# Second passes of a head's two widest score products, each on one half of the array's rows and side by side

## The chip, the core and the metric

The kernel runs on one core of one Trainium2 chip. What is measured is the device time of one execution in microseconds (us). TensorE (PE) multiplies matrices, VectorE (DVE), ScalarE (ACT) and GpSimd (POOL) do the rest, and SyncE (SP) issues every DMA of this kernel from one queue, in the order in which they stand there. A change of over 0.2% either way is about the least that a measurement of this kernel can tell from none.

## What is computed

A decoder trunk of two layers over 512 tokens of width 1024, with 16 heads of 64 dimensions. Layer 0 mixes by stick-breaking attention, layer 1 by dilated softmax attention; each is followed by a SwiGLU feed-forward stage. What matters here are the scores, of which both layers have the same kind:

```
z = jnp.einsum('bhqd,bhkd->bhqk', qb, kh).astype(jnp.float32) * scale   # layer 0, queries in blocks of 128
z = jnp.einsum('brhnqd,brhnkd->brhnqk', qb, k_band).astype(jnp.float32) * scale   # layer 1
```

Both are causal: of the four blocks of 128 queries, block i needs the scores of the first 128 (i + 1) keys alone.

## The kernel before, in words

All operands are float32 numbers kept as two float32r parts, a high and a low one. A product of two such numbers is three products of parts (high by high, high by low, low by high), added up in one PSUM bank; the weights of the model are split in this way on ACT and DVE while they stream in (`raw` tiles, split into `whi` and `wlo`).

For the scores the two parts of a head's 64 dimensions are laid on top of each other. `to_stationary` builds a tile `sta` (`STA[h]`) by DMA, with the high part of the queries in rows 0 to 63 and the low part in rows 64 to 127. `to_moving` builds a tile `mov` (`MOV[h]`) with the keys, high part and low part beside each other, the same in both halves of the rows. So one product on all 128 rows gives the queries' high and low part times one part of the keys at once, and two passes (keys high, keys low) give all four products, low by low among them. Both tiles are made for a pair of heads at a time, by 4 DMAs of `sta` and 4 of `mov`; they come from `hl`, the split query or key projection of the pair. In layer 1 the projection is first rotated (`rope`), which for all pairs but the first takes 4 more DMAs (`rp`) and a product on POOL.

The function `scores(h, u, beside)` issues the score products of one of three units of a head: unit 0 is query block 3 with 512 columns, unit 1 is block 2 with 384, unit 2 is blocks 1 and 0 together. Each unit takes one of three PSUM banks `z`, in turn. `stick_breaking` and `softmax` call it as the first thing of the step W0, W1 or W2 and then turn the scores into weights on ACT and DVE. The order of the steps of a head is written out in `PLAN`: for layer 0 it is T0 W0 F T1 F W1 A0 T2 F A1 W2 F A2, for layer 1 W0 T0 T1 W1 F W2 F A0 T2 F F A1 A2. T are transposes of the weights of the head before (`t<-cst,w` in layer 0, `t<-cst,z` in layer 1), A its products with the values (`av`), and F is filler: pieces of the projections of later heads (`pj`). That order sets priorities; a scheduler then settles the order on each engine by what it expects to be ready, so that a few instructions stand elsewhere than they were written.

Of the kernel before, what the change touches and what calls it, by code (L numbers as in the profile page):

```python
# [7 lines left out]
F = mybir.dt.float32  # L8
# [320 lines left out]
def trunk(ctx, tc, xg, wflat, cst_d, cs_d, outT):  # L329
    nc = tc.nc  # L330
    pe, act, dve, pool, sp = nc.tensor, nc.scalar, nc.vector, nc.gpsimd, nc.sync
# [26 lines left out]
    def T(name, dt=F, k=1):  # L358
        shape = [128, 512] if k == 1 else [128, k, 512]
        return rings["pool"].tile(shape, dt, name=name, bufs=rings["n"][name])  # L360
# [9 lines left out]
    def zb():  # L370
        return ps.tile([128, 512], F, name="z", bufs=3)
# [14 lines left out]
    def mm(out, a, b, start, stop):  # L386
        pe.matmul(out, a, b, start=start, stop=stop, skip_group_check=True)  # L387
# [141 lines left out]
    def to_stationary(p, hl):  # L529
        for i in range(2):  # L530
            t = T("sta", FR)
            for j in range(2):
                sp.dma_start(t[64 * j:64 * j + 64, :].bitcast(F), hl[64 * i:64 * i + 64, j, :].bitcast(F))
            STA[2 * p + i] = t

    def scaled(p):
# [26 lines left out]
    def sta_pieces(layer, p):  # L563

        return proj_pieces(lambda b: to_stationary(p, split_base(position(layer, b, p), 0.125)))
# [60 lines left out]

    UNITS = [[(3, 0, 512)], [(2, 0, 384)], [(1, 0, 256), (0, 256, 256)]]

    def scores(h, u, beside):
        k, q = MOV[h], STA[h]  # L630
        b = zb()
        for j, (i, o, n) in enumerate(UNITS[u]):
            lhs = q[:, 128 * i:128 * i + 128]
            if i == 0 and beside:

                mm(b[:, o:o + 256].rearrange("p (e n) -> p e n", e=2), lhs, k[:, :, :128], False, True)
                continue
            mm(b[:, o:o + n], lhs, k[:, 0, :n], j == 0, False)
            mm(b[:, o:o + n], lhs, k[:, 1, :n], False, True)
        return b  # L640

    def stick_breaking(h, u):

        b = scores(h, u, True)
        n = sum(128 * (i + 1) for i, _, _ in UNITS[u])
        stay, w = T("z"), T("w")
        if u == 2:
            act.activation(stay[:, 384:512], b[:, 384:512], AF.Copy)
            dve.tensor_add(b[:, 256:384], b[:, 256:384], stay[:, 384:512])
        act.activation(stay[:, :n], b[:, :n], AF.Sigmoid, scale=-1.0)  # L650
        act.activation(w[:, :n], b[:, :n], AF.Sigmoid)

        pool.memset(w[:, 128 * (UNITS[u][0][0] + 1) - 1:n:128], 0.0)
        res = {}
        for i, o, _ in UNITS[u]:
            e = o + 128 * (i + 1)
            back = stay[:, o:e][:, ::-1]

            dve.tensor_tensor_scan(back, back, diag[:, 512 - (e - o):][:, ::-1], 0.0, OP.mult, OP.add)
            dve.tensor_mul(w[:, o:e - 1], stay[:, o + 1:e], w[:, o:e - 1])  # L660
            res[i] = w[:, o:e]
        return res

    def softmax(h, u):

        b = scores(h, u, True)
        t = T("z")
        st = sb.tile([128, 4, 2], F, name="st", bufs=6)
        m = len(UNITS[u])
        res = {}  # L670
        for j, (i, o, _) in enumerate(UNITS[u]):
            n = 128 * (i + 1)
            res[i] = t[:, o:o + n]
            m_i = maskB[:, 512 - n:512]
            if i == 0:
                m_i = t[:, o + n:o + 2 * n]
                dve.tensor_add(m_i, b[:, o + n:o + 2 * n], maskB[:, 384:512])
            dve.tensor_tensor_reduce(res[i], b[:, o:o + n], m_i, scale=1.0,
                                     scalar=-3.0e38, op0=OP.add, op1=OP.max, accum_out=st[:, 0, j:j + 1])
        dve.tensor_scalar(st[:, 1, :m], st[:, 0, :m], -1.0, None, op0=OP.mult)  # L680
        for j, (i, _, _) in enumerate(UNITS[u]):
            act.activation(res[i], res[i], AF.Exp, bias=st[:, 1, j:j + 1], accum_out=st[:, 2, j:j + 1])
        dve.reciprocal(st[:, 3, :m], st[:, 2, :m])
        for j, (i, _, _) in enumerate(UNITS[u]):
            if u in DVE_UNITS:
                dve.tensor_scalar(res[i], res[i], st[:, 3, j:j + 1], None, op0=OP.mult)
            else:
                act.activation(res[i], res[i], AF.Copy, scale=st[:, 3, j:j + 1])
        return res
# [60 lines left out]
    def mixer(layer, slot0, gain_next):  # L750
        vslot = lambda p: (slot0 + p) % 9
        oslot = lambda p: (slot0 + 8 + p) % 9
        with phase(f"at{layer}", B_RINGS if layer else A_RINGS):
            def whole(fs_done):
                for f in fs_done[0]:
# [3 lines left out]
            pair = [pjbank(), pjbank()]  # L759
            both("qk", pair)  # L760
            ends = [lambda: to_stationary(0, split_base(position(layer, pair[0], 0), 0.125)),
                    lambda: to_moving(0, split_base(position(layer, pair[1], 0), 1.0))]
            v_first, v_last = v_pieces(0, vslot, zbank)
# [394 lines left out]
```

## Time and profile before

| | |
|---|---|
| median of 3 runs | 1211.41 us (1210.93 to 1211.87) |
| profiled execution | 1214.94 us |
| its span, first to last instruction | 1213.0 us |
| PE busy | 1188.7 us, 98% of the span |
| attention of layer 0 / layer 1, from its first score product on | 37.7 to 228 us / 630 to 826 us |
| score products (`z<-mov,sta`) | 7 a head, 224 in all |

PE's matmuls are pipelined: the recorded durations of neighbours overlap, and the time that one takes of a busy PE is read from its start to the start of the next. In the timeline neighbours of one kind are merged into a row ("x2"), whose first number is the start of the first, and whose second goes to the end of the last. Ends of matmuls are modelled by the profiler.

### The profile page before, as it was taken

The numbers are of one execution on the slowest core, as the hardware profiler recorded it, in microseconds if no ns is written. First come the engines' busy times: TensorE is split into PE (matmuls) and PEld (weight loads), VectorE is DVE, ScalarE is ACT, GpSimd is POOL, SyncE is SP. The second block draws the span as 40 slices with busy tenths as digits, with TensorE's granted clock in tenths as the row PEclk, the third lists the DMA queues.
The fourth block names the chain that finished last, engine by engine and source line by source line (L and its number), as shares of the span: only waits on it lengthen the run. The fifth ranks groups of instructions, "written<-read, shape, count | busy, mean of one in ns | idle before, by whom it ended". The sixth has DMA issues, their size and how long they took to land.

```text
span 1213.0 us, 21104 instructions
## 1 busy us (share of the span) xinstructions
PE 1188.7 (98%) x7501; PEld 1062.5 (88%) x7501; DVE 1013.3 (84%) x1831; ACT 697.2 (57%) x1331; POOL 169.9 (14%) x237
## 2 busy tenths in 40 slices
PE   9999999999999999999999999999999999999997
PEld 7989988888999999998788888888889999999996
DVE  6799899899987878786768899788899878787865
ACT  6667676675544444454466677767755444444443
POOL 0000000001100000014134343110111000000111
PEclk9999999999999999999999999999999999999998
DMA  7654644234242333332154546551343333332122
GB/s 263 179 144 117 154 118 118 62 104 139 89 139 85 109 94 114 90 111 79 35 140 131 155 130 172 144 148 53 96 140 113 114 102 108 91 119 88 44 62 70
DMA packets 74360, 138.30 MB, mean 114 GB/s; under 512 B 9616, under 2 KB 13712, under 8 KB 74256
## 3 DMA queue, kind: packets, MB, share of 16 engines
q1 hardware_dynamic: 74256, 136.97, 39.4%
q8 instruction: 59, 0.97, 0.3%
q14 instruction: 45, 0.37, 0.1%
HBM read 106.00 MB, written 2.10 MB: 89 GB/s over the span
## 4 chain that ended last, share of the span: by engine, by line
PE 86%; DVE 6%; DMA 2%; ACT 2%; issue 2%; POOL 1%; SPq 0%; POOLq 0%; DVEq 0%
PE pj L387 40%; PE z L387 29%; PE t L387 11%; PE av L387 3%; PE t L700 3%; DMA mov<-hl 1%; DMA raw<-wflat 1%; DVE w2lo L307 1%; DVE wlo L307 1%; DVE H L748 1%; ACT whi L306 0%; DVE ACC L441 0%; POOL up L963 0%; DMA H<-xg 0%; POOL H L1071 0%
## 5 line engine op out<-in xcount | busy, mean ns | idle before, releaser
L306 ACT ACTIVATE whi<-raw 128x512 fp32r<-128x512 f32 (+1 forms) x290 | 178.2, 620 | 135.6 <-PE pj L387 53.7
L307 DVE TENSOR_TENSOR wlo<-raw,whi 128x512 fp32r<-128x512 f32 (+1 forms) x290 | 203.6, 710 | 26.7 <-ACT whi L306 24.5
L387 PE MATMUL pj<-VO,whi 128*128 128x512 f32 x568 | 180.7, 398 | 2.0 <-DVE H L748 2.0
L387 PE MATMUL pj<-X,whi 128*128 128x512 f32 x512 | 165.0, 402 | 1.7 <-DVE H L748 1.5
L963 POOL TENSOR_TENSOR up<-up,R 128x512 f32<-128x512 f32 x40 | 61.0, 1528 | 494.7 <-DVE up L1011 443.5
L387 PEld LDWEIGHTS pj<-VO,whi 128*128 128x128 f32 x568 | 102.4, 189 | 24.6 <-issue 2.8
L387 PE MATMUL pj<-VO,wlo 128*128 128x512 f32 x284 | 112.7, 397 | 0.0
L387 PEld LDWEIGHTS pj<-X,whi 128*128 128x128 f32 x512 | 93.0, 189 | 22.2 <-issue 2.0
L748 DVE TENSOR_TENSOR H<-H,pj 128x512 f32<-128x512 f32 (+1 forms) x120 | 79.2, 663 | 32.4 <-PE pj L387 31.7
L387 PE MATMUL pj<-X,wlo 128*128 128x512 f32 x256 | 101.5, 397 | 0.4 <-DVE wlo L307 0.4
L387 PE MATMUL z<-XT,whi 128*128 128x256 f32 x560 | 99.7, 280 | 0.0
L306 ACT ACTIVATE w2hi<-raw 128x512 fp32r<-128x512 f32 (+1 forms) x102 | 62.6, 616 | 60.2 <-PE z L387 18.0
L387 PE MATMUL z<-X,whi 128*128 128x256 f32 (+1 forms) x464 | 96.7, 301 | 0.0
L387 PEld LDWEIGHTS z<-XT,whi 128*128 128x128 f32 x560 | 86.2, 189 | 0.7
L387 PE MATMUL pj<-VO,w2hi 128*128 128x512 f32 x264 | 83.1, 396 | 0.4 <-ACT VO L969 0.4
L307 DVE TENSOR_TENSOR w2lo<-raw,w2hi 128x512 fp32r<-128x512 f32 (+1 forms) x102 | 71.7, 705 | 12.0 <-ACT w2hi L306 11.7
L387 PEld LDWEIGHTS z<-X,whi 128*128 128x128 f32 x464 | 74.9, 189 | 4.8
L387 PE MATMUL z<-XT,wlo 128*128 128x256 f32 x280 | 78.5, 280 | 0.0
L387 PE MATMUL pj<-whi,X 128*128 128x256 f32 x384 | 76.4, 288 | 1.7 <-DVE rp L555 1.7
L387 PE MATMUL z<-XT,w2hi 128*128 128x256 f32 x400 | 75.0, 287 | 2.2 <-ACT s L998 1.2
L387 PE MATMUL z<-X,wlo 128*128 128x256 f32 (+1 forms) x232 | 69.8, 301 | 0.0
L305 POOL TENSOR_TENSOR raw<-raw,H 128x512 f32<-128x512 f32 x48 | 55.8, 1173 | 83.6 <-DMA raw<-wflat 59.0
(202 smaller groups left out, 3018.8 us busy)
## 6 DMA issues: line engine op xcount, KB each, us to landing
raw<-wflat SPq DMA_DIRECT2D x384, 256.0 KB, 2.8
mov<-hl SPq DMA_DIRECT2D x64, 256.0 KB, 4.4
sta<-hl SPq DMA_DIRECT2D x64, 128.0 KB, 2.3
rp<-rp SPq DMA_DIRECT2D x56, 64.0 KB, 2.1
raw<-wflat SPq DMA_DIRECT2D x16, 128.0 KB, 2.4
H<-xg SPq DMA_DIRECT2D x7, 256.0 KB, 5.4
outT<-H SPq DMA_DIRECT2D x2, 512.0 KB, 3.1
CS<-cs SPq DMA_DIRECT2D x1, 512.0 KB, 3.5
```

The source lines that it names most:

```text
L305: nc.gpsimd.tensor_mul(v3, v3, g.unsqueeze(2).to_broadcast([128, n // m, m]))
L306: nc.scalar.activation(hi[:, :n], v, AF.Copy)
L307: nc.vector.tensor_sub(lo[:, :n], v, hi[:, :n].bitcast(F))
L387: pe.matmul(out, a, b, start=start, stop=stop, skip_group_check=True)
L700: pe.transpose(b[:, o:o + 128], pr[i][:, 128 * c:128 * c + 128], idf)
L748: dve.tensor_add(H[:, n, e], H[:, n, e], p[:, e])
L963: pool.tensor_mul(two(u), two(u), r)
```

## The change

It has two parts. In `to_stationary`, the columns 384 to 511 of `sta` (query block 3) get their parts the other way round: low part in rows 0 to 63, high part in rows 64 to 127. Each DMA of 64 rows by 512 columns becomes two, of 384 and of 128 columns.

In `scores`, the call for unit 0 now issues the products of units 0 and 1: the first passes of both on all rows, then the second pass of unit 0 on rows 64 to 127 alone and the second pass of unit 1 on rows 0 to 63 alone, which are the rows that hold the queries' high part. The call for unit 1 only hands over the bank. In these two units the product low by low is no longer formed. Unit 2 is as before.

```
     def to_stationary(p, hl):
         for i in range(2):
             t = T("sta", FR)
+
             for j in range(2):
-                sp.dma_start(t[64 * j:64 * j + 64, :].bitcast(F), hl[64 * i:64 * i + 64, j, :].bitcast(F))
+                for c, part in ((slice(0, 384), j), (slice(384, 512), 1 - j)):
+                    sp.dma_start(t[64 * j:64 * j + 64, c].bitcast(F), hl[64 * i:64 * i + 64, part, c].bitcast(F))
             STA[2 * p + i] = t
...
     UNITS = [[(3, 0, 512)], [(2, 0, 384)], [(1, 0, 256), (0, 256, 256)]]
 
+    ahead = {}
+
     def scores(h, u, beside):
         k, q = MOV[h], STA[h]
+        if u == 0:
+
+            banks = [zb(), zb()]
+            for b, ((i, _, n),) in zip(banks, UNITS):
+                mm(b[:, :n], q[:, 128 * i:128 * i + 128], k[:, 0, :n], True, False)
+            for b, ((i, _, n),), rows in zip(banks, UNITS, (slice(64, 128), slice(0, 64))):
+                mm(b[:, :n], q[rows, 128 * i:128 * i + 128], k[rows, 1, :n], False, True)
+            ahead[h] = banks[1]
+            return banks[0]
+        if u == 1:
+            return ahead.pop(h)
         b = zb()
```

On PE, in layer 0, the scores of head 3 of before stand like this; `z<-mov,sta 128x512` is unit 0, `128x384` unit 1, and the line number is that of the helper `mm`:

```order
277 L387 MATMUL z<-mov,sta 128x512 x2
278 L387 MATMUL pj<-X,whi 128x512 x2
279 L387 MATMUL pj<-X,wlo 128x512
280 L387 MATMUL pj<-X,whi 128x512 x2
281 L387 MATMUL pj<-X,wlo 128x512
282 L700 MATMUL t<-cst,w 128x128 x3
283 L387 MATMUL pj<-X,whi 128x512 x2
284 L387 MATMUL pj<-X,wlo 128x512
285 L387 MATMUL pj<-X,whi 128x512 x2
286 L387 MATMUL pj<-X,wlo 128x512
```

The two products of unit 1 follow four rows further down, at row 291. In the changed kernel the same head reads:

```order
282 L715 MATMUL t<-cst,w 128x128 x3
283 L387 MATMUL z<-mov,sta 128x512
284 L387 MATMUL z<-mov,sta 128x384
285 L387 MATMUL z<-mov,sta 128x512
286 L387 MATMUL z<-mov,sta 128x384
287 L387 MATMUL pj<-X,whi 128x512 x2
288 L387 MATMUL pj<-X,wlo 128x512
289 L387 MATMUL pj<-X,whi 128x512 x2
290 L387 MATMUL pj<-X,wlo 128x512
291 L715 MATMUL t<-cst,w 128x128 x3
```

Unit 1 has moved up beside unit 0, and the third and fourth product of the four are the ones on half of the rows. In 30 of the 32 heads the four stand side by side like this; in two heads of layer 1 the scheduler puts other products between them.

On SP's queue, at the start of layer 1 of before, the DMAs stand in this order (`sta` and `mov` of the first pair, then weights, then the `rp` of the next pair):

```order
128 L243 DMA raw<-wflat 128x512 x16
129 L533 DMA sta<-hl 64x512 x4
130 L526 DMA mov<-hl 64x1024 x4
131 L243 DMA raw<-wflat 128x512 x4
132 L554 DMA rp<-rp 32x512 x4
133 L243 DMA raw<-wflat 128x512
134 L554 DMA rp<-rp 32x512
```

and in the changed kernel in this one:

```order
182 L243 DMA raw<-wflat 128x512 x16
183 L535 DMA sta<-hl 64x384
184 L535 DMA sta<-hl 64x128 x2
185 L535 DMA sta<-hl 64x384 x2
186 L535 DMA sta<-hl 64x128
187 L535 DMA sta<-hl 64x384
188 L535 DMA sta<-hl 64x128
189 L526 DMA mov<-hl 64x1024 x4
190 L243 DMA raw<-wflat 128x512 x4
191 L556 DMA rp<-rp 32x512 x4
```

Eight DMAs of `sta` stand ahead of `mov` where there were four. A later pair of layer 1 (its third) has its `sta` between the `rp` DMAs of the keys; of before:

```order
143 L243 DMA raw<-wflat 128x512 x2
144 L533 DMA sta<-hl 64x512 x4
145 L554 DMA rp<-rp 32x512 x4
146 L243 DMA raw<-wflat 128x512 x2
147 L554 DMA rp<-rp 32x512 x4
148 L243 DMA raw<-wflat 128x512
149 L526 DMA mov<-hl 64x1024 x4
```

and of the changed kernel:

```order
208 L556 DMA rp<-rp 32x512 x2
209 L535 DMA sta<-hl 64x384
210 L535 DMA sta<-hl 64x128 x2
211 L535 DMA sta<-hl 64x384 x2
212 L535 DMA sta<-hl 64x128
213 L535 DMA sta<-hl 64x384
214 L535 DMA sta<-hl 64x128
215 L556 DMA rp<-rp 32x512 x2
```

Two of the four `rp` now stand ahead of the eight `sta`, and two behind them.

## Rows read from the trace of the kernel before

**Rows 1.** The page: PE's busy time, and the chain that ended last

```profile
PE 1188.7 (98%) x7501; PEld 1062.5 (88%) x7501; DVE 1013.3 (84%) x1831; ACT 697.2 (57%) x1331; POOL 169.9 (14%) x237
PE 86%; DVE 6%; DMA 2%; ACT 2%; issue 2%; POOL 1%; SPq 0%; POOLq 0%; DVEq 0%
PE pj L387 40%; PE z L387 29%; PE t L387 11%; PE av L387 3%; PE t L700 3%; DMA mov<-hl 1%; DMA raw<-wflat 1%; DVE w2lo L307 1%; DVE wlo L307 1%; DVE H L748 1%; ACT whi L306 0%; DVE ACC L441 0%; POOL up L963 0%; DMA H<-xg 0%; POOL H L1071 0%
```

**Rows 2.** Windows, both attentions: length, PE, PEld, DVE, ACT, POOL, PEclk, DMA, GB/s

```profile
37.70:228.00 190.30, 190.30 (x1106) 166.26 (x1105) 171.74 (x307) 129.80 (x267) 9.91 (x78) 1.00 0.49 130
630.00:826.00 196.00, 191.22 (x1086) 165.59 (x1087) 167.71 (x433) 136.98 (x317) 59.40 (x73) 0.99 0.56 148
```

**Rows 3.** Waits of PE, attention of layer 1: total us, times, longest

```profile
PE z L387 <- DMA mov<-hl: 1.5, 3, 0.8
PE z L387 <- issue: 1.0, 1, 1.0
```

**Rows 4.** Timeline of PE, head 3 of layer 0: start us, us, instruction, count

```profile
72.70 0.49 PE L700 MATMUL t<-cst,w 128*128 128x128 f32 x3
72.94 0.72 PE L387 MATMUL pj<-X,whi 128*128 128x512 f32 x2
73.50 0.40 PE L387 MATMUL pj<-X,wlo 128*128 128x512 f32 x1
73.73 0.63 PE L387 MATMUL pj<-X,whi 128*128 128x512 f32 x2
...
75.83 0.51 PE L387 MATMUL z<-mov,sta 128*128 128x384 f32 x2
76.19 0.28 PE L387 MATMUL av<-ah,VO 128*128 128x256 f32 x1
```

**Rows 5.** Timeline of PE, head 5 of layer 0, four transposes and what follows

```profile
100.77 0.60 PE L700 MATMUL t<-cst,w 128*128 128x128 f32 x4
101.12 0.37 PE L387 MATMUL pj<-whi,X 128*128 128x256 f32 x1
101.32 0.28 PE L387 MATMUL pj<-wlo,X 128*128 128x256 f32 x1
```

**Rows 6.** Lines by form, score products and their weight loads: busy us, mean ns

```profile
L387 PE MATMUL z<-mov,sta 128*128 128x512 f32 x64 | 21.7, 420 | 2.6 <-DMA mov<-hl 1.5 <-issue 1.0
L387 PE MATMUL z<-mov,sta 128*128 128x384 f32 x64 | 17.6, 354 | 0.0
L387 PEld LDWEIGHTS z<-mov,sta 128*128 128x128 f32 x224 | 36.9, 189 | 7.2 <-issue 2.6 <-PE pj L387 1.4
```

**Rows 7.** Timeline of SP's queue, two stretches of layer 1

```profile
622.07 2.40 SPq L533 DMA_DIRECT2D sta<-hl  x4
625.86 3.16 SPq L526 DMA_DIRECT2D mov<-hl  x4
...
674.77 2.76 SPq L533 DMA_DIRECT2D sta<-hl  x4
677.62 2.45 SPq L554 DMA_DIRECT2D rp<-rp  x4
...
686.72 3.21 SPq L526 DMA_DIRECT2D mov<-hl  x4
```

**Rows 8.** Timeline of PE, first scores of layer 1, with idle time and releaser

```profile
629.04 0.39 PE L387 MATMUL pj<-X,wlo 128*128 128x512 f32 x1
630.47 1.05 PE L387 MATMUL z<-mov,sta 128*128 128x512 f32 x4 [1.03 <-issue]
```

**Rows 9.** Timeline of POOL, layer 1, the rotation of the third pair's keys

```profile
681.62 1.46 POOL L556 TENSOR_TENSOR rp<-rp,CS 128x512 f32<-128x512 f32 x1 [3.47 <-DMA rp<-rp]
```

**Rows 10.** Waits of SP's queue, its longest: total us, times, longest

```profile
SPq L243 <- DVE wlo L307: 400.5, 168, 24.2
```

## Prediction

> **What bounds the kernel now.** I read the page first: PE is busy 98% of the span, and the chain that ended last lies on PE for 86% of it [rows 1]. Then the two attentions, the only stages that the change touches, in windows: in layer 0 PE is busy for all of its 190.3 us and waits for nothing, at the full granted clock; in layer 1 it is busy 191.2 of 196.0 us [rows 2], and the waits of PE there name the landing of `mov`, 1.5 us in three waits, and 1.0 us more before a score product for which the profile shows no releaser [rows 3]. VectorE, at 171.7 and 167.7 us [rows 2], has some 20 us to spare in each. So whatever PE saves or loses in layer 0 goes into the time, and in layer 1 too, as long as `mov` is there when PE arrives. The count of columns that PE streams, and what it loses between products, is the first thing to price; the second is SP's queue, because it brings `mov`.
>
> **What a product costs.** From start to start, a product of 512 columns takes 73.73 - 73.50 = 0.23 us, and the two of 384 columns of a head take 76.19 - 75.83 = 0.36 us, 0.18 each [rows 4]. Their recorded durations are longer, 0.40 us for the 512 and 0.51 for the two of 384 [rows 4]; what sticks out past the start of the next is 0.40 - 0.23 = 0.17 and 0.51 - 0.36 = 0.15 us. I call it the tail, and take 0.16: the time for which a product is still in the array, or on its way through it, while the next one already runs. The weight load before each score product takes 0.19 us [rows 6] and is hidden, since the products follow each other at 0.18 and 0.23.
>
> **The change part by part.**
>
> *Removed:* nothing in number, since a head still has four products for units 0 and 1. But the second pass of unit 1, 384 columns, now lies beside the second pass of unit 0, 512 columns, on the other half of the rows. If both stream at once the longer hides the shorter: 0.18 us a head, 32 x 0.18 = 5.8 us in all. That is the most that the change can give, since nothing else on PE gets shorter.
>
> *Added: two changes of height a head.* The array goes from products on 128 rows to products on 64 and back, 64 times in all. No row of before has a product on 64 rows, so this is bounded by its neighbours. From below: where PE goes from products of float32r parts to float32 transposes and back, it loses nothing. Four transposes and one product of 256 columns take 101.32 - 100.77 = 0.55 us [rows 5], three transposes and two products of 512 take 73.50 - 72.70 = 0.80 [rows 4]; less 0.12 (half of the 0.23) and 0.46 for the products, four transposes take 0.43 and three 0.34, so the fourth costs 0.09 to 0.11 and the three cost three times that, with at most a few hundredths left over for the two changes. But all of these use all 128 rows. From above: the tail runs out before the next kind starts, and its weights are loaded only then, 0.16 + 0.19 = 0.35 us. Between these ends I take the tail, 0.16: a sum over 128 rows that is still running through the array and two separate sums over 64 rows cannot share it as two sums over 128 rows do, and the row that measures what is still in the array when the next product starts is the tail. 64 x 0.16 = 10.2 us. Nothing hides it: in layer 0 PE has no idle time in which it could vanish. The break-even is 0.18 / 2 = 0.09 us a change.
>
> The Trainium skill, "TensorEngine Tiling (Array Packing)", section Tiling Modes, speaks against the change here: switching between tiling modes, though not between tiles of one mode, drains the engine. It gives no figure. By the row on the transposes alone the sum would be a gain, by that rule a loss of the order of the tail, and the trace of before cannot tell, since it holds no second tiling mode. The same skill, "TensorE: Matmul & The Clock Gate", Part 3, reports that products on different row groups start about 4 ns apart and run together; no row here shows it either.
>
> *Moved:* the scores of unit 1 stand at W0, not W1, so their bank is held from there. The bank is asked for again only by the same unit of the next head, a whole head later, so it costs nothing; the time from the transposes of T0 to A0 loses the 0.36 us of unit 1 as cover, but PE shows no wait for `al` or `ah` in layer 0 [rows 2]. If that cover failed, PE would wait for ACT and DVE by up to those 0.36 us a head.
>
> *SP's queue:* 64 DMAs of `sta` more, at 2.40 / 4 = 0.60 us of issue each [rows 7], 2.4 us a pair, on 16 pairs. Queued behind them are weights, `rp` and `mov`. For weights there is room: SP itself waits 400 us for tiles to come free [rows 10]. For `mov` there isn't, in layer 1. First pair: `sta` starts at 622.07, eight take until 626.9, where `mov` went at 625.86 [rows 7]: 1.0 us later. PE already waits there: its product before started at 629.04 and takes 0.23, the first scores start at 630.47 [rows 8], and the order puts as much filler ahead of them as before. So +1.0 us. Third pair: of its four `rp` two now stand behind eight `sta`; POOL's rotation of the keys starts at 681.62 on the landing of `rp` [rows 9], and `mov` goes at 686.72 [rows 7]. If the first two `rp` go at once when `sta` becomes ready, the last goes at about 674.8 + 1.2 + 4.8 + 0.6 = 681.4 and not at 677.62 + 3 x 0.6 = 679.4, 2.0 us later; but the scheduler has put filler and products with the values ahead of those scores, so I take nothing of it, and 2.0 as the upper end. A further pair could lose the whole 2.4. So the queue costs +1.0, with ends at 0 and 5.4.
>
> **Sum.** -5.8 + 10.2 + 1.0 = +5.4 us. On the profiled execution (1213.0 span and 1.9 around it, 1214.94) that makes 1220.3; the median of before is 3.5 us lower than that execution, and the same difference on it gives 1211.4 + 5.4 = 1216.8 us, 0.45% slower.
>
> **The rivals.**
>
> *The change of height is free, or nearly (faster).* For it: the change to transposes and back costs nothing [rows 4, 5]. Against it: those use the same rows. Place: the 64 borders between the first and second passes and behind the latter; it decides below 0.09 us a change, 0.075 with SP's 1.0 us counted. At zero: 1211.4 - 5.8 + 1.0 = 1206.6 us.
>
> *The weights aren't loaded ahead across the border either.* Each change then costs 0.35: 64 x 0.35 = 22.4, less 5.8, plus 1.0, gives 1229.0 us. For it: the load's 0.19 us is as long as the shorter product that hides it. Against it: PEld runs beside PE everywhere in the trace.
>
> *The halves don't run beside each other, so the change doesn't do what it says.* No column is saved: with free changes only SP's 1.0 us is left, 1212.4 us; with the tail at each, 1211.4 + 10.2 + 1.0 = 1222.6.
>
> *`mov` comes late in more pairs of layer 1.* With free changes, -5.8 + 1.0 + 2.0 + 2.4 = -0.4, or 1211.0 us. For it: POOL's wait for `rp` [rows 9]. Against it: the filler put ahead.
>
> **How the numbers follow.** No change that a measurement of this kernel can tell is 0.2%, 2.4 us. The forecast, a change of height at 0.10 to 0.20 us, gives 1213 to 1219.4 and gets 0.42, of which 0.05 lies within 0.2%. Free or nearly free gets 0.27, of which 0.03 lies within. The weights exposed get 0.13. Halves one after the other get 0.10, 0.06 at 1212.4 and 0.04 at 1222.6. Late `mov` with free changes gets 0.08, within 0.2%. So faster 0.24; within 0.05 + 0.03 + 0.06 + 0.08 = 0.22; slower 0.37 + 0.13 + 0.04 = 0.54. The range runs from 1206.2, the free change, to 1223.5, which holds the tail with the queue's upper end (1221.2) and the halves one after the other, and leaves out the weights exposed and the very best of the free case. Both signs have their share in it; the forecast's own range is 1213 to 1219.4.
>
> **What would show it.** In layer 0, where PE is full, the start of the third score product of a head should lie about 0.16 us more than 0.18 behind the start of the second, and the product after the four about 0.16 us more than 0.23 behind that of the third; the fourth should start hardly later than the third. The attention of layer 0 should grow by 16 x (0.32 - 0.18) = 2.2 us. If instead the third follows at 0.18 and the next stage after 0.23, the first rival holds; if the fourth starts only 0.23 behind the third, the halves don't run together; if the gap holds a weight load, the second. In layer 1 the first scores should start about 1 us later against the last of the projections, with `mov` issued at the end of eight `sta`. The forecast is wrong if layer 0 gets shorter; the queue's part is wrong if PE's waits for `mov` in layer 1 grow by more than 3 us or not at all.

## The result, and the profile after

The changed kernel takes 1234.72 us (median of 4 runs, 1233.41 to 1236.22), the kernel before 1211.64 us in the same session (4 runs, 1210.93 to 1213.63): a ratio of 1.018 [1.017, 1.019], 1.8% slower. The sign was forecast, the size was not: 1216.8 us stood there, with a range up to 1223.5. The profiled execution took 1235.01 us, its span is 1233.2 us; of before they were 1214.94 and 1213.0, so 20.2 us of span have to be found.

The page of after, busy times and the chain that ended last, which answer to [rows 1]:

```profile
PE 1200.6 (97%) x7501; PEld 1057.7 (86%) x7501; DVE 1011.5 (82%) x1831; ACT 697.8 (57%) x1331; POOL 175.3 (14%) x237
PE 82%; DVE 7%; DMA 4%; issue 3%; ACT 2%; POOL 1%; SPq 1%; POOLq 0%; DVEq 0%
```

PE is busy for 11.9 us more, and the other 8.3 us are idle time of PE: two losses of different kinds. The chain shows the second, with DMA up from 2% to 4% and SP's queue from 0% to 1%.

Where they lie is read from the first and last score product of each layer. The view of one tile's instructions (count, shortest/median/longest ns, first to last start; then the shapes), of before:

```profile
L387 PE MATMUL z<-mov,sta x112: 277/335/481, 37.9 to 223.6; 128*128 128x256 f32 x48, 128*128 128x512 f32 x32, 128*128 128x384 f32 x32
L387 PE MATMUL z<-mov,sta x112: 274/336/522, 630.5 to 824.4; 128*128 128x256 f32 x48, 128*128 128x512 f32 x32, 128*128 128x384 f32 x32
```

and of after:

```profile
L387 PE MATMUL z<-mov,sta x112: 278/338/503, 41.1 to 230.7; 128*128 128x256 f32 x48, 128*128 128x512 f32 x16, 128*128 128x384 f32 x16, 64*128 64x512 f32 x16
L387 PE MATMUL z<-mov,sta x112: 278/387/792, 637.9 to 844.7; 128*128 128x256 f32 x48, 128*128 128x512 f32 x16, 128*128 128x384 f32 x16, 64*128 64x512 f32 x16
```

The stage in layer 0 grows from 185.7 to 189.6 us (+3.9), the one in layer 1 from 193.9 to 206.8 (+12.9). The first scores come 3.2 us later, the stretch between the two stages is 0.3 us longer, and what follows the last scores is as long as it was. Five products of filler, of 512 columns each, stand behind the first scores in before and ahead of them in after (195 products of PE ahead of the first score there, 200 here). They take 5 x 0.23 = 1.2 us, so for equal work the first scores come 2.0 us later and layer 0 grows by 5.1 us. The greater part lies in layer 1, where I had expected 2.2 us of PE and 1.0 of the queue.

Windows of after, columns as in [rows 2]: layer 0, three stretches of layer 1, and layer 1 from its first to its last scores:

```profile
37.70:230.00 192.30, 191.45 (x1086) 159.62 (x1085) 169.18 (x300) 126.31 (x261) 9.92 (x77) 1.00 0.50 131
...
639.00:642.40 3.40, 3.40 (x10) 2.84 (x11) 1.40 (x7) 1.42 (x4) 1.04 (x1) 0.51 0.91 304
...
671.70:676.60 4.90, 4.89 (x14) 3.44 (x14) 2.51 (x14) 1.76 (x5) 1.75 (x2) 0.50 0.58 154
...
714.10:717.50 3.40, 3.40 (x18) 3.40 (x17) 1.86 (x2) 2.34 (x6) 2.08 (x3) 0.51 0.45 116
...
637.90:844.70 206.80, 196.98 (x1078) 163.34 (x1079) 162.75 (x428) 134.40 (x311) 62.29 (x73) 0.97 0.53 139
```

and of before, a stretch of layer 1, and layer 1 cut at its own first and last scores:

```profile
643.30:646.70 3.40, 3.40 (x18) 3.40 (x17) 3.27 (x11) 2.06 (x4) 1.06 (x1) 0.51 0.71 171
...
630.50:824.40 193.90, 189.59 (x1078) 164.19 (x1079) 165.67 (x429) 134.89 (x313) 59.40 (x73) 0.99 0.56 147
```

In layer 0 PE is still busy nearly throughout at the full clock. In layer 1 its idle time grows from 193.9 - 189.6 = 4.3 to 206.8 - 197.0 = 9.8 us, and its busy time by 7.4 us. Three stretches of it run at the lower of PE's two clocks, 1.2 and not 2.4 GHz (granted 0.50 to 0.51), where before had one. Waits of PE in layer 1, against [rows 3]:

```profile
PE z L387 <- issue: 4.7, 1, 4.7
PE z L387 <- DMA mov<-hl: 3.0, 3, 2.5
```

The 2.5 us are the first pair's, the 4.7 us lie ahead of the first scores of the second pair; before, the first pair had waited 1.0 us [rows 8] and the second 0.3.

**Four score products of a head.** PE in head 4 of layer 0 of after, the first line the two on half of the rows:

```profile
86.51 0.49 PE L387 MATMUL z<-mov,sta 64*128 64x512 f32 x2
86.93 0.72 PE L387 MATMUL pj<-X,whi 128*128 128x512 f32 x2
87.50 0.39 PE L387 MATMUL pj<-X,wlo 128*128 128x512 f32 x1
```

and the weight loads beside them:

```profile
86.51 0.19 PEld L387 LDWEIGHTS z<-mov,sta 64*128 64x128 f32 x2 [0.31 <-issue]
86.93 0.30 PEld L387 LDWEIGHTS pj<-X,whi 128*128 128x128 f32 x2 [0.23 <-issue]
```

The two on half of the rows end 0.49 us after the first one's start, though one alone lasts that long: they run side by side. But from there to the next product it is 86.93 - 86.51 = 0.42 us where 0.23 would do, and the two `pj` behind take 87.50 - 86.93 = 0.57 and not 0.46. The weight load of the new height (86.51, 86.93) starts with the product and not ahead of it. In before the products follow each other at 0.18 and 0.23 us [rows 4], so their loads of 0.19 us [rows 6] run beside the product ahead.

**SP's queue in layer 1.** After, against [rows 7]; the first pair's `sta` and `mov`, then the second pair's:

```profile
628.06 4.95 SPq L535 DMA_DIRECT2D sta<-hl  x8
633.11 3.23 SPq L526 DMA_DIRECT2D mov<-hl  x4
...
651.53 5.52 SPq L535 DMA_DIRECT2D sta<-hl  x8
657.09 1.66 SPq L556 DMA_DIRECT2D rp<-rp  x1
...
666.79 3.62 SPq L526 DMA_DIRECT2D mov<-hl  x4
```

The second pair of before, which I had not shown:

```profile
643.20 2.43 SPq L533 DMA_DIRECT2D sta<-hl  x4
645.68 1.22 SPq L554 DMA_DIRECT2D rp<-rp  x2
...
655.16 3.18 SPq L526 DMA_DIRECT2D mov<-hl  x4
```

and the two instructions of DVE that `mov` hangs on there:

```profile
652.97 0.68 DVE L557 TENSOR_TENSOR rp<-rp 128x512 f32<-128x512 f32 x1
...
654.35 0.75 DVE L513 TENSOR_TENSOR hl<-rp,hl 128x512 fp32r<-128x512 f32 x1
```

Timelines of POOL, DVE and PE of after, in the order in which the work passes from one to the next:

```profile
660.30 1.29 POOL L558 TENSOR_TENSOR rp<-rp,CS 128x512 f32<-128x512 f32 x1 [3.61 <-DMA rp<-rp]
```

```profile
661.62 0.69 DVE L559 TENSOR_TENSOR rp<-rp 128x512 f32<-128x512 f32 x1 [2.48 <-POOL rp L558]
662.23 2.44 DVE L601 TENSOR_TENSOR VO<-s,VO 128x256 fp32r<-128x256 f32 x2
664.60 1.52 DVE L307 TENSOR_TENSOR wlo<-raw,whi 128x512 fp32r<-128x512 f32 x1
666.05 0.68 DVE L513 TENSOR_TENSOR hl<-rp,hl 128x512 fp32r<-128x512 f32 x1
```

```profile
666.65 0.40 PE L387 MATMUL pj<-X,whi 128*128 128x512 f32 x1
671.71 2.75 PE L387 MATMUL z<-mov,sta 128*128 128x512 f32 x7 [4.67 <-issue]
674.25 0.63 PE L387 MATMUL pj<-X,whi 128*128 128x512 f32 x1
674.68 0.63 PE L387 MATMUL pj<-X,wlo 128*128 128x512 f32 x1
```

This is the whole chain: the last `rp` of the keys stands behind eight `sta`, POOL waits 3.6 us for it, DVE 2.5 us for POOL, then `hl` comes behind three other DVE instructions (4.4 us behind `rp` from start to start, where before it was 1.4), and only then `mov` is issued, at 666.79. PE has been out of other work since 671.71 - 4.67 = 667.04. The profile calls its wait "issue", but it ends 1.3 us after the last of the four `mov` has been issued (666.79 + 3.62 = 670.41), so I read it as a wait for them. And then PE runs slowly: at 674.25 a product of 512 columns takes 0.43 us to the next and not 0.23, and the granted clock in the window 671.7 to 676.6 is 0.50, the lower of the two levels.

### The profile page after: what moved, and what is told of

It is laid out like the page before. It is cut to its first block, busy times and chain, and to the rows that moved or that the text cites. A ratio compares the mean times of both kernels' runs of the same rounds, so it can differ in the third digit from the quotient of the medians.

```text
span 1233.2 us, 21181 instructions
## 1 busy us (share of the span) xinstructions
PE 1200.6 (97%) x7501; PEld 1057.7 (86%) x7501; DVE 1011.5 (82%) x1831; ACT 697.8 (57%) x1331; POOL 175.3 (14%) x237
## 4 chain that ended last, share of the span: by engine, by line
PE 82%; DVE 7%; DMA 4%; issue 3%; ACT 2%; POOL 1%; SPq 1%; POOLq 0%; DVEq 0%
PE pj L387 38%; PE z L387 28%; PE t L387 11%; PE av L387 3%; PE t L715 3%; DMA mov<-hl 2%; DMA raw<-wflat 1%; DVE wlo L307 1%; DVE H L763 1%; DVE w2lo L307 1%; ACT whi L306 0%; DMA H<-xg 0%; DVE X L420 0%; POOL H L1086 0%; DMA rp<-rp 0%
## 5 line engine op out<-in xcount | busy, mean ns | idle before, releaser
L307 DVE TENSOR_TENSOR wlo<-raw,whi 128x512 fp32r<-128x512 f32 (+1 forms) x290 | 206.4, 718 | 31.6 <-ACT whi L306 26.6
L387 PE MATMUL pj<-X,whi 128*128 128x512 f32 x512 | 168.9, 410 | 2.5 <-DVE H L763 1.5
L307 DVE TENSOR_TENSOR w2lo<-raw,w2hi 128x512 fp32r<-128x512 f32 (+1 forms) x102 | 71.4, 702 | 11.8 <-ACT w2hi L306 11.5
L305 POOL TENSOR_TENSOR raw<-raw,H 128x512 f32<-128x512 f32 x48 | 59.3, 1246 | 88.9 <-DMA raw<-wflat 60.0
L721 ACT ACTIVATE ah<-t 128x384 fp32r<-128x384 f32 (+1 forms) x96 | 49.4, 526 | 38.7 <-PE t L715 37.9
```

Of the source, the lines that this page charges most:

```text
L305: nc.gpsimd.tensor_mul(v3, v3, g.unsqueeze(2).to_broadcast([128, n // m, m]))
L307: nc.vector.tensor_sub(lo[:, :n], v, hi[:, :n].bitcast(F))
L721: act.activation(hi[:, s:e], b[:, s:e], AF.Copy)
```

## The experiments

Layer lengths are from the first to the last score product in the profiled execution. Ratios are to runs of before in the same session.

| run | median, us | ratio [95%] | layer 0 | layer 1 |
|---|---|---|---|---|
| before | 1211.64 | | 185.7 | 193.9 |
| after | 1234.72 | 1.0181 [1.0169, 1.0193] | 189.6 | 206.8 |
| e1_dmas_only | 1227.71 | 1.0111 [1.0086, 1.0137] | 185.0 | 204.7 |
| e2_halves_four_dmas | 1219.95 | 1.0048 [1.0033, 1.0062] | 190.4 | 194.5 |
| e3b_same_half | 1223.85 | 1.0091 [1.0074, 1.0109] | 192.4 | 196.6 |
| e4b_moved_only | 1215.93 | 1.0022 [1.0013, 1.0031] | 188.2 | 191.6 |
| e5_after_act_queue | 1257.09 | 1.0350 [1.0317, 1.0382] | 211.4 | 208.1 |
| e7_dmas_act_queue | 1246.12 | 1.0273 [1.0255, 1.0290] | 208.1 | 202.6 |
| e8_dmas_behind_rp | 1213.45 | 0.9999 [0.9987, 1.0011] | 185.0 | 190.2 |
| e9_before_behind_rp | 1210.40 | 0.9976 [0.9963, 0.9988] | 185.6 | 189.7 |
| e10_four_changes | 1235.33 | 1.0186 [1.0169, 1.0202] | 197.8 | 201.5 |
| e11_moved_in_layer_1 | 1213.74 | 1.0000 [0.9990, 1.0011] | 185.7 | 191.9 |
| e12_after_behind_rp | 1221.24 | 1.0071 [1.0055, 1.0087] | 189.4 | 190.4 |

### Taking the change apart: the eight DMAs alone, the halves alone

The first run puts the eight DMAs of `sta` into the kernel before and leaves its products as they were. The products then still run on all rows, where the order of the two parts makes no difference.

```
# on the kernel before
-                sp.dma_start(t[64 * j:64 * j + 64, :].bitcast(F), hl[64 * i:64 * i + 64, j, :].bitcast(F))
+                for c, part in ((slice(0, 384), j), (slice(384, 512), 1 - j)):
+                    sp.dma_start(t[64 * j:64 * j + 64, c].bitcast(F), hl[64 * i:64 * i + 64, part, c].bitcast(F))
```

> The kernel before with the DMAs of the stationary tile alone changed: eight for a pair of heads in place of four, with the parts of query block 3 the other way round; all score products stay on 128 rows, in their old places. Theory A (two causes: each change of the array's height costs 0.19 us, 32 x (0.38 - 0.18) = 6.5 us, and the other 16.6 us of the loss are keys that come late behind eight DMAs in layer 1): 1211.6 + 16.6, some 1225 to 1230 us, with layer 0 as long as before. Theory B (the DMAs cost about 1 us, as predicted, and the loss in layer 1 comes from the products themselves and their new places): 1212 to 1213 us.

Measured: 1.1% slower, 13.5 us by the ratio (10.4 to 16.6), of the change's 21.9 us. In the profiled execution layer 1 is 10.8 us longer. The first scores come 1.3 us later, of which 1.2 are the five products of filler named above, and for equal work layer 0 is 0.5 us longer. The stretch ahead of layer 1's scores is 2.8 us longer: 1.4 more of waiting for the first pair's `mov`, and 3.4 us at the lower clock at 300 us, which cost 1.7. Its rows show the same chain as those of after, with no product on half of the rows in the program. SP, POOL and PE of this run:

```profile
648.12 5.00 SPq L534 DMA_DIRECT2D sta<-hl  x8
653.16 0.61 SPq L555 DMA_DIRECT2D rp<-rp  x1
...
663.72 3.54 SPq L526 DMA_DIRECT2D mov<-hl  x4
```

```profile
657.25 1.29 POOL L557 TENSOR_TENSOR rp<-rp,CS 128x512 f32<-128x512 f32 x1 [3.71 <-DMA rp<-rp]
```

```profile
668.53 1.83 PE L387 MATMUL z<-mov,sta 128*128 128x512 f32 x4 [4.61 <-issue]
```

The second run is the change with the four DMAs of before; the columns of query block 3 then hold their parts the old way round, so for them the second pass multiplies the queries' low part by the keys' low part where the high part belongs.

```
-                for c, part in ((slice(0, 384), j), (slice(384, 512), 1 - j)):
-                    sp.dma_start(t[64 * j:64 * j + 64, c].bitcast(F), hl[64 * i:64 * i + 64, part, c].bitcast(F))
+                sp.dma_start(t[64 * j:64 * j + 64, :].bitcast(F), hl[64 * i:64 * i + 64, j, :].bitcast(F))
```

> The changed kernel with the four DMAs of before: the second passes run on half of the rows each and side by side, but in block 3 the rows used hold the queries' low part, so low by low is formed there in place of high by low. Theory A: only the array's part is left, 1211.6 + 6.5 = 1218 us, with 0.2 us more a head in layer 0 and no wait for keys in layer 1 beyond those of before. Theory B: nearly the whole loss stays, 1231 to 1234 us.

Measured: 0.5% slower, 5.8 us (4.0 to 7.5). With the 13.5 of the first run that makes 19.3 of 21.9, within the intervals: the two parts add up, and the DMAs are the larger one. The 5.8 us hold the halves and the move of unit 1's scores together; a run further down has the move alone.

### PE's part: side by side, and the price of a change of height

Both second passes on the same half of the rows, one behind the other, with four DMAs. In the first version of this run and of the next one, the edit by a slip also reached `fold`, which takes the halves of the `av` bank; both were run again without it. In the first versions an odd head's outputs are so put together from the wrong rows. Their ratios were 1.0078 [1.0054, 1.0102] and 1.0006 [0.9992, 1.0021]; the repeats stand in the table.

```
-            for b, ((i, _, n),), rows in zip(banks, UNITS, (slice(64, 128), slice(0, 64))):
+            for b, ((i, _, n),), rows in zip(banks, UNITS, (slice(0, 64), slice(0, 64))):
```

> As the kernel with halves and four DMAs, but both second passes on rows 0 to 63, so that they can't stand side by side (low by low is not formed in these units; both use the high part of block 2 and block 3 alone). If the gain of standing side by side is real, the fourth product starts 0.23 us behind the third and the kernel is 32 x 0.18 = 5.8 us slower than the one with different halves, some 1224 us by theory A. If the two halves in truth share the array's time, the two kernels are equal.

> The kernel with halves and four DMAs, with both second passes on rows 0 to 63, the queries' high part, and so not side by side; low by low is not formed in these two units. If standing side by side really gives time, the fourth product starts 0.23 us behind the third, not 0.003, and the kernel is up to 32 x 0.18 = 5.8 us slower than with different halves; what PE loses in layer 1 may hide in its waits for keys. If the halves share the array's time, the two are equal.

PE of the repeat, its two products on half of the rows and the one behind them:

```profile
84.58 0.50 PE L387 MATMUL z<-mov,sta 64*128 64x512 f32 x1
...
84.92 0.34 PE L387 MATMUL z<-mov,sta 64*128 64x384 f32 x1
85.18 0.50 PE L387 MATMUL pj<-X,whi 128*128 128x512 f32 x1
```

On one half the second starts 0.34 us behind the first; on two halves it started with it. From the third product to the one behind the four it is 85.18 - 84.58 = 0.60 us and not 0.42: 0.18 a head. The run is 0.43% above the second run, 5.2 us (some 2.4 to 8, by the intervals of the two ratios, each to its own session), against the 5.8 us that I had put on running side by side. The gain is there, and of the size that was worked out.

The rows also split the price. The first product after the change takes 0.34 us and not 0.23, which is 0.11 more, and the last one before the change back 0.26 and not 0.18, 0.08 more. Over the 16 heads of layer 0 of this run the means are 0.09 us ahead of the first product of a new height and 0.10 between it and its follower, the same on the way down and on the way up: 0.195 us a change. I read the 0.09 as an array that waits for the old height to leave, and the 0.10 as what sticks out of a weight load of 0.19 us that only starts with the product; no run separates the two.

The counterpart keeps all products on all rows and only moves them:

```
-            for b, ((i, _, n),), rows in zip(banks, UNITS, (slice(64, 128), slice(0, 64))):
+            for b, ((i, _, n),), rows in zip(banks, UNITS, (slice(0, 128), slice(0, 128))):
```

> As the kernel with halves and four DMAs, but the second passes on all 128 rows (all four products of parts, as before): only the move of unit 1's scores beside unit 0's is left. Theory A: within 2 us of before, 1210 to 1214 us. Theory B, if the new places cost time: over 1215 us.

> The kernel with halves and four DMAs, with the second passes on all 128 rows: the move of unit 1's scores beside unit 0's alone. Both theories now say within 2 us of before, since the kernel with halves and four DMAs is only 6 us slower than before in all; over 3 us would mean that the places and not the changes of height cost that time.

Measured: 0.2% slower, 2.6 us (1.6 to 3.8). Layer 0 is 2.5 us longer, of which 1.3 us are waits of PE that before had not (0.9 for DVE's `H`, 0.4 ahead of score products); the rest is not assigned to a line. Layer 1 is shorter by 2.3 us; some 1.7 of that is before's stretch at the lower clock, which the profiled execution of this run hasn't there. The next run asks whether that is a gain: the move in layer 1 alone.

```
# on e4b_moved_only
-    def scores(h, u, beside):
+    def scores(h, u, beside, both=False):
...
-        if u == 0:
+        if both and u == 0:
...
# in softmax
-        b = scores(h, u, True)
+        b = scores(h, u, True, True)
```

> The kernel before with the scores of unit 1 moved beside those of unit 0 in layer 1 alone, all on 128 rows. In the kernel with this move in both layers layer 1 was some 2 us shorter and layer 0 some 2 us longer from the first to the last score product. If that was no chance, this one takes 1208 to 1211 us; if it was, 1211 to 1214 us.

Measured: no difference over 12 runs, with a layer 1 of 191.9 us. So the 2 us of that stage in one profiled execution are no time won for the whole, and the 2.6 us of the move in both layers go with layer 0.

Last, twice the changes: whole, half, whole, half.

```
# on the second run's kernel
             banks = [zb(), zb()]
-            for b, ((i, _, n),) in zip(banks, UNITS):
+            for b, ((i, _, n),), rows in zip(banks, UNITS, (slice(64, 128), slice(0, 64))):
                 mm(b[:, :n], q[:, 128 * i:128 * i + 128], k[:, 0, :n], True, False)
-            for b, ((i, _, n),), rows in zip(banks, UNITS, (slice(64, 128), slice(0, 64))):
                 mm(b[:, :n], q[rows, 128 * i:128 * i + 128], k[rows, 1, :n], False, True)
```

> The kernel with halves and four DMAs, with the products of a head in the order whole, half, whole, half: four changes of height a head and not two, and no two halves side by side. If each change costs 0.19 us and standing side by side gives 0.18, layer 0's score products take 16 x (0.38 + 0.18) = 9 us longer from first to last, 199 us after 190, and the kernel is 12 to 18 us slower than with two changes, 1232 to 1238 us. If what costs is not the change but, say, the half-height products as such, it takes what the same-half kernel takes, 1224 us.

PE of this run, head 4 of layer 0, the second to the fourth of the four:

```profile
86.46 0.50 PE L387 MATMUL z<-mov,sta 64*128 64x512 f32 x1
...
86.89 0.44 PE L387 MATMUL z<-mov,sta 128*128 128x384 f32 x1
...
87.26 0.44 PE L387 MATMUL z<-mov,sta 64*128 64x384 f32 x1
```

They start 0.43 and 0.37 us apart, where 0.23 and 0.18 would be without a change: 0.20 and 0.19 a change again. The run is 1.9% slower than before, 22.6 us (20.5 to 24.5), within what was expected. Against the kernel with both second passes on one half (e3b_same_half), where nothing runs side by side either, two changes a head are all that is added: it is 0.95% above that one, 11.5 us (some 8.6 to 14.5), for 64 x 0.195 = 12.5. So it is the changes that cost, and not the products on half of the rows as such. Layer 0 is 7.4 us longer than in the second run. Two more changes a head and the overlap lost make 16 x (2 x 0.195 + 0.18) = 9.1 us; where the other 1.7 us went wasn't found.

### The queue's part: place or number

Two theories were left for the DMAs: their place, ahead of the `rp` that the keys wait for (C), or their number, as traffic that delays others wherever it stands (D). The first try moved the eight DMAs of `sta` from SP's queue to ACT's, in after and in the first run's kernel.

```
-                    sp.dma_start(t[64 * j:64 * j + 64, c].bitcast(F), hl[64 * i:64 * i + 64, part, c].bitcast(F))
+                    act.dma_start(t[64 * j:64 * j + 64, c].bitcast(F), hl[64 * i:64 * i + 64, part, c].bitcast(F))
```

> The changed kernel with the eight DMAs of the stationary tile issued from ACT's queue and not from SP's; nothing is left out. Theory C (what costs is the time that SP spends on issuing eight DMAs ahead of rp and mov): layer 1 falls back to about 194 us from its first to its last score product, and the kernel to that with four DMAs, about 1218 to 1221 us. Theory D (the smaller transfers themselves are late, or slow the others on the DMA engines): it stays at 1230 to 1235 us. ACT blocked by its own issuing would lie between.

> The kernel before with the eight smaller DMAs of the stationary tile, issued from ACT's queue; all score products on 128 rows in their old places. Theory C: back to about 1212 us, at most a few us over it for what ACT loses. Theory D: 1225 to 1228 us, as with the eight on SP.

Measured: 3.5% and 2.7% slower, which neither theory expected. The waits of ACT in layer 0 of the second of these runs, its queue and its instruction behind it say why:

```profile
ACT z L651 <- DMA sta<-hl: 32.7, 6, 6.2
...
72.96 5.01 ACTq L534 DMA_DIRECT2D sta<-hl  x8
78.01 0.49 ACT L651 ACTIVATE z<-z 128x384 f32<-128x384 f32 x1 [5.09 <-DMA sta<-hl]
```

ACT does none of its own work for 32.7 us ahead of its first instruction on a block of scores. It is not waiting for data there: the 5.09 us of the row are the 5.01 us in which it issues eight DMAs, some 0.6 us each. Layer 0 alone grows by some 22 us. That is a new loss and tells nothing of C or D.

So the DMAs stayed on SP's queue, and only their place was changed: in layer 1 the `sta` of a pair is issued when the `rp` of the same pair's keys have been. Here on the first run's kernel, with eight DMAs:

```
+    held = []
...
         for g in range(4):
             sp.dma_start(sw[32 * g:32 * g + 32, :], t0[32 * (g ^ 1):32 * (g ^ 1) + 32, :])
+        while held:
+            to_stationary(*held.pop())
...
     def sta_pieces(layer, p):
-        return proj_pieces(lambda b: to_stationary(p, split_base(position(layer, b, p), 0.125)))
+        def done(b):
+            hl = split_base(position(layer, b, p), 0.125)
+            if layer:
+                held.append((p, hl))
+            else:
+                to_stationary(p, hl)
+        return proj_pieces(done)
```

> The kernel before with the eight smaller DMAs of the stationary tile (all score products on 128 rows), but in layer 1, from the second pair on, they are issued from SP behind the rp DMAs of the same pair's keys, not between or ahead of them. As many DMAs and as much issue time on SP as with eight before. Theory C (the eight delay the rp, and through the rotation the keys' mov): layer 1's score products, 205 us from first to last with eight ahead, take 194 to 198 us, and the kernel 1214 to 1221 us. Theory D (the number of transfers or SP's total issue time costs, wherever they stand): 1225 us or more.

Its queue, at the second pair:

```profile
645.24 1.77 SPq L556 DMA_DIRECT2D rp<-rp  x3
648.66 6.39 SPq L535 DMA_DIRECT2D sta<-hl  x8
...
656.47 3.11 SPq L527 DMA_DIRECT2D mov<-hl  x4
```

Measured: as fast as before, 0.9999 [0.9987, 1.0011], with the same eight DMAs a pair that cost 1.1% in the other place, and a layer 1 of 190.2 us and not 204.7. So theory D, that the number costs wherever the DMAs stand, falls for the greater part of the 13.5 us, and theory C, the place, holds. What is not separated is how much of that lies in the queue alone, since the scheduler also lays the work beside it differently: of the second pair's keys, `hl` starts 4.4 us behind `rp` on DVE in the two kernels with eight DMAs ahead, and 1.4 to 1.5 us behind it in before, in the second run and in the three with the DMAs behind. No run holds that order fixed.

The same edit on the kernel before, with its four DMAs, and on after:

> The kernel before with its four DMAs of the stationary tile put behind the rp DMAs in the same way, nothing else. If SP's queue holds the keys back in the kernel before too, layer 1 gets shorter by up to 3 us, 1208 to 1211 us. If in the kernel before PE's waits for keys come from the rotation on DVE and ACT, it stays at 1211 to 1214 us.

```profile
640.80 1.77 SPq L555 DMA_DIRECT2D rp<-rp  x3
642.67 2.78 SPq L534 DMA_DIRECT2D sta<-hl  x4
...
648.91 3.25 SPq L527 DMA_DIRECT2D mov<-hl  x4
```

`mov` of the second pair goes 6.2 us earlier than before (648.91 against 655.16), and the kernel takes 1210.40 us over 11 runs, 0.24% less than before [0.12%, 0.37%], within the first of the two ranges. It is the only version here that beats both kernels, if by little. It is also the counterpart of the run with eight DMAs in that place, which is 0.23% slower, 2.8 us (1.4 to 4.1): so four more DMAs are not quite free there. Behind the `rp` they stand from layer 1's second pair on alone; at the first pair the eight still stand ahead of `mov`, and PE's wait for it is 2.4 us and not 1.1.

> The changed kernel as it is, with its eight DMAs of the stationary tile put behind the rp DMAs of the same pair's keys in layer 1. If its loss is the sum of the two causes (eight DMAs ahead of rp; two changes of height a head less what the halves save side by side), only the second is left, as in the kernel with halves and four DMAs: layer 1's score products some 194 us from first to last, the kernel 1218 to 1221 us. If the two together cost something that neither does alone, it stays above 1223 us.

Measured: 0.7% slower, 8.6 us (6.7 to 10.5), where the change as it was lost 21.9. Its layer 1, from first to last scores:

```profile
637.70:828.10 190.40, 189.84 (x1078) 159.39 (x1079) 161.49 (x428) 133.64 (x311) 58.35 (x73) 1.00 0.57 151
```

PE is idle for 0.6 us of that stage, at the full clock. The loss that is left fits the run with four DMAs (5.8 us, 4.0 to 7.5). It can't be found piece by piece in this trace: the profiled execution is the fastest of the six, at 1217.69 us, with a granted clock of 0.997 on the mean where the others have 0.994 to 0.995. The first scores start at 37.5 to 38.3 us in every profiled run with four DMAs on SP's queue, and at 39.2 to 41.1 in every one with eight; 1.2 us of that are the five products of filler, which are not lost.

## Why the prediction was wrong in size and right in sign

**Side by side, -5.8 us: right.** The third and fourth product start together (86.51), and taking it away cost 0.18 us a head in the rows and 5.2 us in the run. The Trainium skill, "TensorE: Matmul & The Clock Gate", Part 3, says that tiles on different row groups start some 4 ns apart; this trace agrees, with about 3 ns.

**Changes of height, +10.2 us: right in kind, a little too small.** I took 0.16 us out of bounds of 0 to 0.35; it is 0.195. So the term is 64 x 0.195 = 12.5 us, and with the -5.8 us PE loses 6.7 and not 4.4 us by the rows. The rival of the free change falls. The rival in which the weights aren't loaded ahead was half right: they aren't, but all that a change loses is 0.195 us and not 0.35, of which 0.09 stand ahead of the first product. That my 0.16 came near is luck: I had read it as the tail, from ends that the profiler models, and left the weight load out. The Trainium skill, "TensorEngine Tiling (Array Packing)", section Tiling Modes, says that switching modes drains the engine; the trace agrees in so far as a switch costs 0.195 us here.

**The move, 0 us: too little.** I let it cost nothing. The move alone cost 2.6 us (1.6 to 3.8), with 1.3 us of waits in layer 0, for DVE's `H` and ahead of scores, and not for `al` or `ah`, which I had looked at. The run with the halves and four DMAs holds this too, so the halves by themselves cost it some 3.2 us (1.1 to 5.2) and not 6.7. Of the difference 0.8 us is found: PE's waits in layer 0 are 0.5 us there and not 1.3. That its 5.8 us lie near my 4.4 is therefore in part luck. Layer 0 of the change grew by 3.9 us, 5.1 for equal work, for a forecast of 2.2.

**SP's queue, +1.0 us with an upper end of 5.4: this step failed.** It measured 13.5 us (10.4 to 16.6) by itself. What I had priced came out: the first pair's wait for `mov` grew from 1.03 to 2.46 us, 1.4 for 1.0. Three choices were wrong.

First, the pair. I priced the first pair, whose `mov` stood directly behind, and looked at the third, and took no row of the second. There the time that counts is not `mov`'s place in the queue but that of the last `rp`, from which POOL, two instructions of DVE and only then `mov` follow. Before, PE waited for it by 0.3 us already; it had no reserve. PE's longest wait in that stage of before, 1.7 us for an `rp` of DVE at 642, isn't among [rows 3] either.

Second, the size. I let a pair lose at most its own extra issue time, 2.4 us. The eight `sta` of the second pair take 5.5 us to be issued, where the four took 2.4, and the last `rp` then takes 1.7. Measured against the first scores of the layer, the last `rp` was issued through 4.5 us later than before, POOL began its rotation 2.3 us later, DVE its `rp` 1.3 us later, and `mov` was issued 4.2 us later. So slack on the way took up most of the queue's delay, and DVE, where three instructions and not one now stand between `rp` and `hl`, made 3.0 us of it new. Filler didn't cover it: PE ran out of it at 667.0.

Third, what follows a stall. I counted waits alone. After the first pair's wait of 2.5 us, the second's of 4.7 and two shorter ones near 713 the clock was granted at its lower level for a while. In the three windows that costs 1.7, 2.4 and 1.7 us, against 1.7 in before, behind a wait of 1.7: 4.1 us more. So layer 1 adds up: 5.5 us of idle time, 3.4 us for the changes of height less the overlap, 4.1 us of clock, 13.0 for the 12.9 us. Not every such wait is followed by the lower clock: the kernel with eight DMAs behind the `rp` and the changed kernel with them there wait 2.4 and 2.5 us at the first pair too, and the granted clock stays at 1.00.

The rival "`mov` comes late in more pairs" had the right mechanism and, in POOL's wait for `rp` [rows 9], the right row, only for a pair later than the one that decided. I gave it 4.4 us and tied it to free changes of height, so it came out at 1211.0 us; in the range its 4.4 us stand only as 1221.2, which did not move the upper end. The sign I named for the failure of this term, waits for `mov` grown by more than 3 us, is what happened: 2.5 us in the two rows of before [rows 3] are 7.7 us now.

**What is left open.** The first scores of the run come 3.2 us later: 1.2 are the five products of filler, and a granted clock of 0.86 in the first 12 us of the profiled execution of after, which neither before nor the first run shows there, makes up to 1.7 more. In layer 0 the move alone cost 2.5 us in one execution, half of it not assigned, and most of the difference between 6.7 and 3.2 us for the halves isn't either. How much of the queue's 13.5 us the order on DVE makes, no run tells.

## What to carry to other kernels

When a change adds DMAs to a queue, don't price their issue time but follow each transfer behind them to the engine that waits for it, for every pair or round and not the first alone, and put those that nobody waits for soon behind those that feed a chain: the same eight DMAs made the kernel 1.1% slower in one place and no slower in another. Follow the order on the engines of that chain too, since a scheduler may answer a new delay with a new order. Products on half of the rows pay only if what a visit saves, here 0.18 us, exceeds two changes of height, here 0.39. A stall of PE costs more than its length when the clock is granted lower behind it.

## What the runs showed of the hardware

A change of height between products costs 0.195 us, 0.09 of it ahead of the first product of the new height and 0.10 behind it, with a weight load that starts only with the product. Between products of one height none of this is lost, and to the transposes nothing in the sum: three of them and the two products behind take 0.80 us [rows 4]. Two products on different halves of the rows run at once without slowing each other (0.49 us for both, 0.50 for one alone). After waits of 2.5 and 4.7 us in after and of 1.7 us in before PE worked at the lower of its two clocks for 3.4, 4.9 and 3.4 us, with 0.43 us for a product that otherwise takes 0.23; other waits of 2.4 and 2.5 us were not followed by it. And DMAs issued by ACT hold up ACT's own work: issuing eight takes it 5.0 us, and 33 us of its time in layer 0 went that way.
